# Strassen-Winograd FFN pairs: PSUM banks of a tile declared independent, and three columns done in the plain form

## The chip, the cores and the metric

The kernel runs on one core of a Trainium2 chip. The metric is the device time of one execution in microseconds (us); lower is better. Each core has a matrix engine (TensorE, PE in the profile, with its weight loads shown as PEld), a vector engine (VectorE, DVE), a scalar engine (ScalarE, ACT), GpSimd (POOL), and a queue engine (SyncE, SP) that issues the DMAs here. Matmul results go to PSUM, which has 8 banks of 512 fp32 values per partition. A PSUM tile of this kernel is 128 x 1024 fp32, two banks.

## The reference

Two transformer-like blocks on x of 1024 tokens by 1024 channels, all in fp32. What matters here is the last stage of the second block, a gated feed-forward network with a causal convolution of three taps between its two products:

```
z = rmsnorm(x) @ w_up                     # 1024 x 1024 by 1024 x 5632
zc = conv_b + sum over 3 taps of conv_w[tap] * z shifted by tap
gate, val = halves of zc                  # 2816 channels each
x = x + (silu(gate) * val) @ w_down       # 2816 x 1024
```

The 2816 gate channels are 22 columns of 128; column f of the gate and column f of val (f + 22 in `w_up`) make one of 22 tasks.

## The kernel before, in words

Precision: each fp32 operand is split into two fp32r numbers, hi (a ScalarE copy) and lo (VectorE: source minus hi; `hilo`, line 126 for the subtraction), and each product is three matmuls: hi by hi, lo by hi, hi by lo (`mm3`). A matmul is 128 x 128 weights by 512 columns of tokens.

Order: the kernel is a list of slots (`run`). A slot has weights, matmuls (`mm`), an epilogue (`epi`), and may take background tasks (`bg`: so many from the queue `bgq` after its matmuls; -1: all that are left) or work ahead of its matmuls (`mid`). Every engine executes its instructions in the order in which this list traces them. Weights of plain slots are loaded one or two slots ahead by SP (`dma_ahead`, tile `wr`), split by ScalarE and VectorE into `wh` and `wl` (`split_ahead`, two buffers each). `hold` on a slot sets `self.limit`, the number of weight requests that may be loaded before somebody lifts it.

Plain form of an FFN column: `mm_std`, 2 token halves x 8 blocks of channels x 3 matmuls = 48 for the gate and 48 for val, 96 together. Its epilogue `up_epi` runs `up_tasks`: ScalarE scales and biases the PSUM tile into `z`, VectorE adds two taps from PSUM (line 129), then silu (gate) or the product of gate and val, which SP writes to DRAM (`G_sp`, line 1643).

Columns 0 (gate and val) and 1 (gate) are done in half slots of 24 matmuls (`next_half_slots`, names uh0.0 to uh2.1), the first of them among the last slots of the stage before; up1.1 is a plain slot. Then come the pairs.

Pair form (`run_two`, columns 2 to 21 before): the product of two weight columns (gate and val) with the two token halves is done after Strassen and Winograd with 7 products in place of 8. Each product is 4 blocks x 3 matmuls = 12, so 84 for a pair. The weights' raw tile `raw` (`two_load`, line 311) gives sums (`two_sums`), and four parts a, b, c, d are split to hi and lo (`two_hi`, line 336, and `two_lo`); the tokens' sums are made once by `sums_of`, 16 background tasks in four groups of whole, first, second and split (tiles `f`, `s`, and the results in `A` and `B`), taken by the half slots. Products go into four banks, g1 and g2 of tile x, g3 and g4 of tile y. In order, with what VectorE and ScalarE do:

1. product 1 into g1 (weights a); ScalarE copies g1 to `e[:, 0]` (tile `two`)
2. product 6 into g2 (b); VectorE: `e[:, 1]` = g2 + `e[:, 0]`
3. product 5 into g3 (b); VectorE: `e[:, 2]` = g3 - `e[:, 0]`
4. product 2 onto g1 (a)
5. product 7 onto g2 (c); VectorE: g4 = `e[:, 2]` - g2
6. product 3 onto g3 (d); VectorE: g3 = g3 - `e[:, 1]`
7. product 4 onto g2 (c); VectorE: g2 = g2 + `e[:, 0]`

The texts below number the products by this order of issue, 1 to 7. The epilogue of a pair (`todo`) is woven into the next pair by `old`; the last pair runs its own at once. In the trace `wa`, `wb`, `wc` are the parts a, b, c, and part d lies in the tiles `A` and `B`, which also hold the tokens' hi and lo.

The way out: in the last pair `last_two` opens the pools of the plain form again in the place of wa and wb, and loads the first weights of the down projection. Then `open_d` loads the first gate products (`gr`), and `down` runs 2 x 22 column steps of 24 matmuls (names dn0.0 onward; the last two of each half in one slot) into all 8 PSUM banks.

Of the kernel before, what the change touches and what calls it, by code (L numbers as in the profile page):

```python
# [12 lines left out]
R = mybir.dt.float32r  # L13
AF = mybir.ActivationFunctionType
ALU = mybir.AluOpType
AX = mybir.AxisListType

S = 1024
D = 1024
NK = 8  # L20
H = 512
P = 128
NF = 22
# [50 lines left out]
class Kernel:  # L74
# [32 lines left out]
        self.c1 = self.ca.enter_context(self.pool(name, reuse_waits="tile"))  # L107

    def mul(self, *a, **k):
        self.nc.tensor.matmul(*a, **k)  # L110

    def flip(self, *a):
        self.nc.tensor.transpose(*a)  # L113
# [1 line left out]
    def act(self, out, in_, func=AF.Identity, bias=None, scale=None, accum=None):  # L115
        kw = {}
        if bias is not None:
            kw["bias"] = bias
        if scale is not None:
            kw["scale"] = scale  # L120
        if accum is not None:
            kw["accum_out"] = accum
        self.nc.scalar.activation(out, in_, func, **kw)  # L123

    def tt(self, out, a, b, op):
        self.nc.vector.tensor_tensor(out, a, b, op)  # L126

    def stt(self, out, a, s, b, op0, op1):
        self.nc.vector.scalar_tensor_tensor(out, a, s, b, op0, op1)  # L129
# [42 lines left out]

    def mm3(self, out, a, b, first, last, **k):
        (ah, al), (bh, bl) = a, b
        self.mul(out, ah, bh, start=first, stop=False, **k)
        self.mul(out, ah, bl, start=False, stop=False, **k)
        self.mul(out, al, bh, start=False, stop=last, **k)

    def mm_std(self, ps, w, xh, xl, nk=NK, k0=0, halves=(0, 1), xk0=0):
        wh, wl = w  # L180
# [175 lines left out]
    def run_two(self, n):  # L356
        t = self.twos[n]
        x, y = self.pair(), self.pair()
        g1, g2, g3, g4 = x[:, :H], x[:, H:], y[:, :H], y[:, H:]
        later = deque(self.twos[n - 1].todo if n else ())  # L360
        e = self.c1.tile([P, 3, H], F, tag="two", name="two")

        def product(out, op, which, off, first):
            (wh, wl), (xh, xl) = t.__dict__[which], self.X7[op]
            for k in range(4):
                ws = slice(off + k * P, off + (k + 1) * P)
                self.mm3(out, (wh[:, ws], wl[:, ws]), (xh[:, k], xl[:, k]),
                         first and k == 0, k == 3, skip_group_check=True)

        def old(k):  # L370
            for _ in range(min(k, len(later))):
                later.popleft()()

        product(g1, 1, "a", 0, True)
        self.two_hi(n, "c")
        old(2)
        self.act(e[:, 0], g1)
        product(g2, 6, "b", 0, True)
        old(1)
        self.two_lo(n, "c")  # L380
        self.two_hi(n, "d")
        self.tt(e[:, 1], g2, e[:, 0], ALU.add)
        product(g3, 5, "b", H, True)
        self.two_lo(n, "d")
        self.two_hi(n + 1, "a")
        self.two_sums(n + 1, 0)
        self.tt(e[:, 2], g3, e[:, 0], ALU.subtract)
        product(g1, 2, "a", H, False)
        if n == len(self.twos) - 1:
            self.last_two()  # L390
        self.two_load(n + 2)
        self.two_sums(n + 1, 1)
        self.two_lo(n + 1, "a")
        old(1)
        product(g2, 7, "c", 0, False)
        self.two_hi(n + 1, "b")
        old(2)
        self.tt(g4, e[:, 2], g2, ALU.subtract)
        product(g3, 3, "d", 0, False)
        self.two_lo(n + 1, "b")  # L400
        old(1)
        self.tt(g3, g3, e[:, 1], ALU.subtract)
        product(g2, 4, "c", H, False)
        old(len(later))
        self.tt(g2, g2, e[:, 0], ALU.add)
        t.todo = t.epi(x, y)
        if n == len(self.twos) - 1:
            for f in t.todo:
                f()
# [514 lines left out]
    def out_phase(self, blk):  # L924
        nc, I = self.nc, self.I
# [111 lines left out]
        def norm(t):  # L1037
            x, v = X[t], V[t]
            nc.vector.tensor_scalar(x, x, v[:, 0:1], v[:, 1:2], ALU.add, ALU.mult)
            self.tt(x, x, st["ln_g"], ALU.mult)  # L1040
            nc.gpsimd.tensor_tensor(x, x, st["ln_b"], ALU.add)
            nc.sync.dma_start(self.x1_sp[t], x)

        def scale(t):
            y = st["z", t] = self.c1.tile([P, 1024], F, tag="oz", name="oz", bufs=2)
            self.stt(y, X[t], V[t][:, 2:3], st["mix" if ln else "ffn"], ALU.mult, ALU.mult)
# [52 lines left out]
        def flip_slot(t):  # L1099
            add(Slot(mm=lambda: flips(t), name="fl"))  # L1100
# [3 lines left out]
        def then(f, *ts):  # L1104
            add(Slot(epi=lambda: [f(t) for t in ts]))

        nxt = self.next_half_slots(blk)
# [17 lines left out]
        if ln:  # L1125
            add(nxt[0])
            flip_slot(6)
            nxt[1].mid = lambda: norm(7)
            add(nxt[1])
            then(square, 7)  # L1130
            nxt[2].mid = lambda: scale(7)
            add(nxt[2])
            flip_slot(7)
            self.slots.extend(nxt[3:])
        else:
            then(scale, 7)
            add(nxt[0])
            flip_slot(7)
            add(Slot(pre=self.open_ffn))
            for x in nxt[1:]:  # L1140
                x.bg = 4
            self.slots.extend(nxt[1:])

    def next_half_slots(self, blk):
# [81 lines left out]
    def block2(self):  # L1226
# [135 lines left out]
        def att_a(n, kv):  # L1362
# [14 lines left out]
            def epi():  # L1377
# [8 lines left out]
                nm, es, tot = sm[:, 0], sm[:, 1], sm[:, 2]  # L1386
                nc.vector.tensor_reduce(nm, t[:, :, v], AX.X, ALU.max)
                self.tt(nm, nm, self.nslope[:, hs], ALU.mult)
# [205 lines left out]
    def open_ffn(self):  # L1594
        self.reopen("cf", "")
        self.wp = self.c1
        self.sh = [self.big(n, R).rearrange("p k (h t) -> p (k h) t", h=2).rearrange(
            "p (n k) t -> p n k t", n=4) for n in ("B1", "A0")]
        self.G_sp = self.dram.tile([NF, P, 1024], F, name="g_sp")
        wc = [self.wp.tile([P, 1024], R, name="wc%d" % j) for j in range(2)]  # L1600
        wa, wb = [[], []], []
        wd = [self.A1[:, 8192 + i * H:8192 + (i + 1) * H] for i in range(2)]
        count = [0]

        def tile(which):
            if which in "ab" and not wb:
                p, = self.open_right("wab")
                for i in range(2):
                    wa[i] += [p.tile([P, 1024], R, name="wa%d%d" % (i, j)) for j in range(2)]
                wb.extend(p.tile([P, 1024], R, name="wb%d" % j) for j in range(2))  # L1610
            if which == "a":
                count[0] += 1
                return wa[(count[0] + 1) % 2]
            return {"b": wb, "c": wc, "d": wd}[which]

        self.two_tile = tile
        self.X7 = self.operands(*self.H, self.sh)

        def scratch():
            return (self.wp.tile([P, 2, 1024], F, tag="raw", name="f", bufs=2),  # L1620
                    self.wp.tile([P, 4, H], F, tag="sums", name="s"))

        self.bgq.extend(self.sums_of(*self.H, self.sh, scratch))
        self.bgq.append(self.two_begin)
# [28 lines left out]
    def ffn(self):  # L1653
        nc, I = self.nc, self.I

        def mm3up(w):
            self.ps3 = self.pair()
            self.mm_std(self.ps3, w, *self.H)

        self.slots.append(Slot([I["w_up"][1 + NF]], mm3up, mid=self.last_half, bg=-1,  # L1660
                               epi=lambda: self.up_epi(1, 1, self.ps3), name="up1.1"))
        self.slots.append(Slot(pre=self.two_first))
        self.slots.append(Slot(pre=lambda: self.open_psum(4, 0)))

# [4 lines left out]
                return [g[0], g[1], g[2], lambda: (g[3](), v[0]()), v[1], v[2], v[3]]  # L1669
            return epi  # L1670

        for f in range(2, NF):
            slot = Slot(name="up%d" % f)
            slot.two = Two(I["w_up"][f], I["w_up"][f + NF], epi_of(f))
            self.slots.append(slot)
# [3 lines left out]
        def last_two():  # L1679
            _, self.first_g = self.open_right("ws", "g0")  # L1680
            t = st["g", 0, 0] = self.first_g.tile([P, H], F, name="gr0")
            nc.sync.dma_start(t, self.G_sp[0][:, 0:H])
            self.limit += 1
            self.split_ahead()

        self.last_two = last_two

        def down(hf, fs):
            hs = slice(hf * H, (hf + 1) * H)
# [47 lines left out]
            def epi():  # L1737
                if not end:
                    return
                for b in range(8):  # L1740
                    if b == 5 and hf == 0:
# [5 lines left out]

            self.slots.append(Slot([I["w_dn"][f] for f in fs], mm, epi, pre,
                                   split=[lambda f=f: split(f) for f in fs], name="dn%d.%d" % (hf, fs[0])))
            self.slots[-1].hold = True  # L1750

        def open_d():
            self.reopen("cd")
            self.limit = 1 << 30
            for f in range(1, 5):
                t = st["g", 0, f] = self.c1.tile([P, H], F, tag="gr", name="gr", bufs=6)
                nc.sync.dma_start(t, self.G_sp[f][:, 0:H])

        self.slots.append(Slot(pre=open_d))
        for hf in range(2):  # L1760
            for f in range(NF - 2):
                down(hf, (f,))
            down(hf, (NF - 2, NF - 1))
# [83 lines left out]
```

## Time and profile before

| | |
|---|---|
| median of 3 runs | 2848.7 us (2848.11 to 2849.38) |
| the profiled execution | 2853.09 us, span 2851.3 us |
| PE | 2741.4 us busy, 12180 matmuls |
| DVE, ACT | 1565.5 and 862.7 us busy |
| granted clock of PE | 0.99 of full on average |
| pairs | from about 2148 to 2586 us of the span |

The busy time of PE is made of modelled ends of pipelined matmuls, which overlap: a matmul shows 0.39 us of its own while the next starts some 0.23 us after it. Rows of the timeline give start, length, engine, line, operation, output and inputs, and in brackets the idle time before it and who ended it. A line is often that of a helper (110 all matmuls, 126 all two-input VectorE operations), so tiles tell the groups apart.

### The profile page before, as it was taken

What the parts mean: (1) busy time and instruction counts of PE and PEld (TensorE: products, weight loads), DVE (VectorE), ACT (ScalarE), POOL (GpSimd) and SP (SyncE); (2) the same over time, 40 slices, a digit from 0 to 9 for tenths busy, and PEclk for the clock granted to TensorE, in tenths of its full rate; (3) what the DMA queues carried; (4) which work ended last, traced back from release to release, by engine and by line L of the source; (5) the groups of instructions that cost most, each with busy time, mean ns of one, the idle gap of its engine ahead of it and who ended that gap; (6) DMA issues with size and microseconds to landing.
All of it is one profiled execution on the core that took longest, in us unless ns stands there. A gap on an engine that the chain in (4) does not pass through costs nothing.

```text
span 2851.3 us, 29350 instructions
## 1 busy us (share of the span) xinstructions
PE 2741.4 (96%) x12180; PEld 2239.4 (79%) x12180; DVE 1565.5 (55%) x1675; ACT 862.7 (30%) x1102; POOL 137.0 (5%) x131
## 2 busy tenths in 40 slices
PE   5999999999999999999999999999988999997999
PEld 3888888888888888888887888888866777775887
DVE  6898888831335323522662355457466777773343
ACT  6322222211222212411442355433233333332222
POOL 4010000000000000000041100000000000000000
PEclk9999999999999999999999999999989999998999
DMA  5111111122111333221422222024312112112544
GB/s 222 45 67 60 52 52 59 59 75 73 56 48 45 105 132 111 96 81 67 148 95 77 82 74 74 30 90 151 141 58 83 74 67 82 74 63 103 177 171 159
DMA packets 76167, 255.15 MB, mean 89 GB/s; under 512 B 8577, under 2 KB 9089, under 8 KB 76034
## 3 DMA queue, kind: packets, MB, share of 16 engines
q1 hardware_dynamic: 76034, 253.28, 25.1%
q8 instruction: 96, 1.57, 0.2%
q14 instruction: 37, 0.30, 0.0%
HBM read 208.15 MB, written 45.09 MB: 89 GB/s over the span
## 4 chain that ended last, share of the span: by engine, by line
PE 87%; DVE 7%; issue 2%; ACT 2%; DMA 1%; POOL 1%; SPq 0%; DVEq 0%; ACTq 0%; POOLq 0%
PE pp L110 85%; DVE z L129 2%; DVE wa L126 1%; PE pm L110 1%; PE pp L113 1%; PE pm L113 1%; DVE s L126 1%; DVE wl L126 1%; ACT oj L123 0%; DVE pp L126 0%; DVE A L126 0%; DVE two L126 0%; ACT two L123 0%; DVE sums L126 0%; ACT B L132 0%
## 5 line engine op out<-in xcount | busy, mean ns | idle before, releaser
L110 PE MATMUL pp<-A,wh 128*128 128x512 f32 x4192 | 1307.1, 392 | 19.1 <-DVE A L126 8.3
L110 PEld LDWEIGHTS pp<-A,wh 128*128 128x128 f32 x4192 | 786.3, 188 | 191.1 <-DVE A L126 9.9
L110 PE MATMUL pp<-A,wl 128*128 128x512 f32 x2128 | 832.5, 391 | 6.7 <-DVE wl L126 6.6
L126 DVE TENSOR_TENSOR wl<-wr,wh 128x1024 fp32r<-128x1024 f32 (+1 forms) x228 | 274.6, 1205 | 553.4 <-ACT wh L132 551.9
L110 PEld LDWEIGHTS pp<-A,wl 128*128 128x128 f32 x2128 | 401.6, 189 | 93.4 <-DVE wl L126 9.6
L132 ACT CAST wh<-wr 128x1024 fp32r<-128x1024 f32 (+1 forms) x228 | 229.9, 1009 | 423.5 <-PE pp L110 405.9
L129 DVE SCALAR_TENSOR_TENSOR h<-p,par_t,h 128x1024 f32<-128x1024 f32 x240 | 309.4, 1289 | 7.7
L110 PE MATMUL pp<-B,wh 128*128 128x512 f32 x960 | 303.6, 392 | 0.7 <-DVE sy L129 0.7
L110 PEld LDWEIGHTS pp<-B,wh 128*128 128x128 f32 x960 | 181.3, 189 | 38.5 <-issue 0.9
L110 PE MATMUL pp<-B,A 128*128 128x512 f32 x640 | 188.5, 399 | 23.6 <-DVE pp L126 23.2
L110 PE MATMUL pp<-B,wl 128*128 128x512 f32 x448 | 174.3, 389 | 0.0
L110 PEld LDWEIGHTS pp<-B,A 128*128 128x128 f32 x640 | 120.5, 189 | 57.4 <-issue 31.5
L110 PE MATMUL pp<-wh,gh 128*128 128x512 f32 x352 | 138.4, 393 | 15.1 <-ACT gh L132 9.7
L110 PE MATMUL pp<-wl,gh 128*128 128x512 f32 x352 | 138.5, 393 | 0.3 <-DVE wl L126 0.3
L110 PE MATMUL pp<-wh,gl 128*128 128x512 f32 x352 | 138.4, 393 | 0.1
L129 DVE SCALAR_TENSOR_TENSOR z<-pp,par_t,z 128x1023 f32<-128x1023 f32 x88 | 112.7, 1281 | 39.4 <-ACT z L123 37.8
L126 DVE TENSOR_TENSOR mg<-pp,mg 128x1024 f32<-128x1024 f32 x24 | 29.4, 1224 | 168.2 <-PE pp L110 168.2
L110 PE MATMUL pp<-B,wb 128*128 128x512 f32 x320 | 105.7, 402 | 13.8 <-ACT two L123 13.8
L110 PE MATMUL pp<-A,wa 128*128 128x512 f32 x320 | 107.1, 396 | 5.1 <-DVE z L129 4.0
L110 PEld LDWEIGHTS pp<-B,wl 128*128 128x128 f32 x448 | 84.1, 188 | 17.4
L123 ACT ACTIVATE mg<-pp,par_t 128x1024 f32<-128x1024 f32 x24 | 26.8, 1117 | 219.8 <-PE pp L110 219.8
L110 PEld LDWEIGHTS pp<-wh,gh 128*128 128x128 f32 x352 | 66.7, 190 | 30.5 <-ACT gh L132 10.5
(265 smaller groups left out, 2952.6 us busy)
## 6 DMA issues: line engine op xcount, KB each, us to landing
wr<-in_w_in SPq DMA_DIRECT2D x129, 512.0 KB, 3.2
wr<-in_w_dn SPq DMA_DIRECT2D x44, 512.0 KB, 3.4
raw<-in_w_up SPq DMA_DIRECT2D x40, 512.0 KB, 4.5
wr<-in_w_br SPq DMA_DIRECT2D x24, 512.0 KB, 3.5
g_sp<-z SPq DMA_DIRECT2D x22, 512.0 KB, 2.6
gr<-g_sp SPq DMA_DIRECT2D x44, 256.0 KB, 3.8
m_sp<-mg SPq DMA_DIRECT2D x16, 512.0 KB, 2.9
mi<-m_sp SPq DMA_DIRECT2D x16, 512.0 KB, 5.0
```

Of the source, the lines that this page charges most:

```text
L110: self.nc.tensor.matmul(*a, **k)
L113: self.nc.tensor.transpose(*a)
L123: self.nc.scalar.activation(out, in_, func, **kw)
L126: self.nc.vector.tensor_tensor(out, a, b, op)
L129: self.nc.vector.scalar_tensor_tensor(out, a, s, b, op0, op1)
L132: self.nc.scalar.copy(hi, src)
```

## The change

The helpers `mul`, `act` and `tt` return the instruction that they make, and `mm3` a list of three. In `run_two` every instruction of the seven products and of the VectorE and ScalarE steps is noted under its bank. For two instructions on different engines (one of them PE) in different banks of the same tile it is declared that they do not depend on each other; between instructions in the same bank an explicit dependence is added.

Columns 2, 3 and 21 are done in the plain form: 2 and 3 ahead of the pairs and 21 behind them; 17 pairs are left (4 to 20). The 16 background tasks and the first raw loads are taken by the half slots as 2, 2, 1, 1, 1 (4 each before), by the four plain slots that follow as 2 each, and the rest by the last. `last_two` now lifts the limit altogether and splits one weight, that of column 21; `hold` moves from the down slots to the plain slot of column 21. The tiles wa, wb are allocated in an order that depends on the number of pairs.

```diff
     def mm3(self, out, a, b, first, last, **k):
         (ah, al), (bh, bl) = a, b
-        self.mul(out, ah, bh, start=first, stop=False, **k)
-        self.mul(out, ah, bl, start=False, stop=False, **k)
-        self.mul(out, al, bh, start=False, stop=last, **k)
+        return [self.mul(out, ah, bh, start=first, stop=False, **k),
+                self.mul(out, ah, bl, start=False, stop=False, **k),
+                self.mul(out, al, bh, start=False, stop=last, **k)]
...
+        seen = {1: [], 2: [], 3: [], 4: []}
+        other = {1: 2, 2: 1, 3: 4, 4: 3}
+
+        def apart(bank, insts, after=()):
+            for i in insts:
+                for o in seen[other[bank]]:
+                    if (o.ins.engine == PE) == (i.ins.engine == PE):
+                        continue
+                    self.tc.declare_no_dep(i.ins, o.ins, reason="other bank")
+            for o in after:
+                self.tc.add_manual_dep(insts[0].ins, o.ins.name, mybir.DependencyInfo(
+                    mybir.DependencyClass.Sync, mybir.DependencyReason.DATA), reason="same bank")
+            seen[bank] += insts
+
-        def product(out, op, which, off, first):
+        def product(bank, op, which, off, after=()):
             (wh, wl), (xh, xl) = t.__dict__[which], self.X7[op]
+            out, insts = banks[bank], []
             for k in range(4):
                 ws = slice(off + k * P, off + (k + 1) * P)
-                self.mm3(out, (wh[:, ws], wl[:, ws]), (xh[:, k], xl[:, k]),
-                         first and k == 0, k == 3, skip_group_check=True)
+                insts += self.mm3(out, (wh[:, ws], wl[:, ws]), (xh[:, k], xl[:, k]),
+                                  not after and k == 0, k == 3, skip_group_check=True)
+            apart(bank, insts, after)
+            return insts[-1]
+
+        def vec(bank, inst, after):
+            apart(bank, [inst], [after])
+            return inst
...
-        product(g1, 1, "a", 0, True)
+        banks = {1: g1, 2: g2, 3: g3, 4: g4}
+        m1 = product(1, 1, "a", 0)
...
-        self.act(e[:, 0], g1)
-        product(g2, 6, "b", 0, True)
+        c1 = vec(1, self.nc.scalar.copy(e[:, 0], g1), m1)
+        m2 = product(2, 6, "b", 0)
...
-        self.tt(e[:, 1], g2, e[:, 0], ALU.add)
-        product(g3, 5, "b", H, True)
+        v2 = vec(2, self.tt(e[:, 1], g2, e[:, 0], ALU.add), m2)
+        m3 = product(3, 5, "b", H)
...
-        self.tt(e[:, 2], g3, e[:, 0], ALU.subtract)
-        product(g1, 2, "a", H, False)
+        v3 = vec(3, self.tt(e[:, 2], g3, e[:, 0], ALU.subtract), m3)
+        product(1, 2, "a", H, [c1])
...
-        product(g2, 7, "c", 0, False)
+        m2 = product(2, 7, "c", 0, [v2])
...
-        self.tt(g4, e[:, 2], g2, ALU.subtract)
-        product(g3, 3, "d", 0, False)
+        v2 = self.tt(g4, e[:, 2], g2, ALU.subtract)
+        apart(2, [v2], [m2])
+        apart(4, [v2])
+        m3 = product(3, 3, "d", 0, [v3])
...
-        self.tt(g3, g3, e[:, 1], ALU.subtract)
-        product(g2, 4, "c", H, False)
+        vec(3, self.tt(g3, g3, e[:, 1], ALU.subtract), m3)
+        m2 = product(2, 4, "c", H, [v2])
         old(len(later))
-        self.tt(g2, g2, e[:, 0], ALU.add)
+        vec(2, self.tt(g2, g2, e[:, 0], ALU.add), m2)
...
-            for x in nxt[1:]:
-                x.bg = 4
+            for x, n in zip(nxt[1:], (2, 2, 1, 1, 1)):
+                x.bg = n
...
-                for i in range(2):
-                    wa[i] += [p.tile([P, 1024], R, name="wa%d%d" % (i, j)) for j in range(2)]
-                wb.extend(p.tile([P, 1024], R, name="wb%d" % j) for j in range(2))
+                last = (len(self.twos) + 1) % 2
+                for x, i in ((wa[1 - last], "a0"), (wb, "b"), (wa[last], "a1")):
+                    x.extend(p.tile([P, 1024], R, name="w%s%d" % (i, j)) for j in range(2))
...
-        def mm3up(w):
-            self.ps3 = self.pair()
-            self.mm_std(self.ps3, w, *self.H)
-
-        self.slots.append(Slot([I["w_up"][1 + NF]], mm3up, mid=self.last_half, bg=-1,
-                               epi=lambda: self.up_epi(1, 1, self.ps3), name="up1.1"))
+        up = {}
+
+        def plain(f, side, bg=0):
+            def mm(w):
+                up[f, side] = self.pair()
+                self.mm_std(up[f, side], w, *self.H)
+
+            slot = Slot([I["w_up"][f + NF * side]], mm, bg=bg, name="up%d.%d" % (f, side),
+                        epi=lambda: self.up_epi(f, side, up[f, side]))
+            self.slots.append(slot)
+            return slot
+
+        plain(1, 1, 2).mid = self.last_half
+        for f, side, bg in ((2, 0, 2), (2, 1, 2), (3, 0, 2), (3, 1, -1)):
+            plain(f, side, bg)
         self.slots.append(Slot(pre=self.two_first))
...
-        for f in range(2, NF):
+        for f in range(4, NF - 1):
...
             nc.sync.dma_start(t, self.G_sp[0][:, 0:H])
-            self.limit += 1
-            self.split_ahead()
+            self.limit = 1 << 30
+            self.split_ahead(1)

         self.last_two = last_two
+        plain(NF - 1, 0).hold = True
+        plain(NF - 1, 1)
...
-            self.slots[-1].hold = True

         def open_d():
             self.reopen("cd")
-            self.limit = 1 << 30
```

More of the change, by code (lines that the diff above doesn't have):

```diff
@@ L16 @@
 AX = mybir.AxisListType
+PE = mybir.EngineType.PE
 S = 1024
@@ L109, in mul @@
     def mul(self, *a, **k):
-        self.nc.tensor.matmul(*a, **k)
+        return self.nc.tensor.matmul(*a, **k)
     def flip(self, *a):
@@ L122, in act @@
             kw["accum_out"] = accum
-        self.nc.scalar.activation(out, in_, func, **kw)
+        return self.nc.scalar.activation(out, in_, func, **kw)
     def tt(self, out, a, b, op):
-        self.nc.vector.tensor_tensor(out, a, b, op)
+        return self.nc.vector.tensor_tensor(out, a, b, op)
     def stt(self, out, a, s, b, op0, op1):
```

## The prediction

> **What bounds the kernel now.** I read the page first, then the busy time by stretches, then who waited for whom inside the FFN pairs, then the instructions of one pair, then the two ends of the pairs.
>
> ```profile
> span 2851.3 us, 29350 instructions
> PE 2741.4 (96%) x12180; PEld 2239.4 (79%) x12180; DVE 1565.5 (55%) x1675; ACT 862.7 (30%) x1102; POOL 137.0 (5%) x131
> ```
>
> TensorE is the bound, but its 96% hides gaps, because the modelled ends of matmuls overlap what comes next. The number of matmuls in a stretch says more (columns: length, busy time and count of PE, PEld, DVE, ACT, POOL, then the granted clock).
>
> ```profile
> 200.00:400.00 200.00, 200.00 (x884) 165.62 (x883) 168.10 (x135) 47.20 (x44) 19.38 (x16) 1.00 0.17 58
> 2085.00:2150.60 65.60, 47.87 (x170) 35.72 (x169) 49.08 (x43) 21.30 (x18) 0.00 (x0) 0.84 0.19 66
> 2191.40:2553.64 362.24, 333.33 (x1429) 265.38 (x1429) 271.70 (x290) 126.70 (x136) 0.00 (x0) 1.00 0.19 72
> 2553.64:2607.67 54.03, 34.15 (x132) 26.23 (x133) 23.61 (x24) 11.93 (x14) 0.00 (x0) 0.84 0.24 83
> ```
>
> A stretch of plain projections issues 884 matmuls in 200 us: 0.2262 us each, my price of a matmul throughout. The second row is the way into the pairs (170 matmuls, worth 38.5 us, in 65.6), the third is 17 whole pairs, the fourth the way out (132, worth 29.9 us, in 54.0). All three lose time, and the change touches all three.
>
> The steady pairs (who waited for whom: total us, times, longest) and one of them, with the start of the sixth product in two pairs 17 apart:
>
> ```profile
> DVE z L129 <- ACT z L123: 22.7, 17, 1.3
> PE pp L110 <- DVE pp L126: 17.2, 17, 1.0
> DVE two L126 <- PE pp L110: 16.1, 34, 0.7
> PE pp L110 <- ACT two L123: 11.7, 17, 0.7
> ...
> 2191.40 8.46 PE pp L110 x36
> 2553.64 8.46 PE pp L110 x36
> ...
> 2306.00 0.39 PE L110 MATMUL pp<-A,wa 128*128 128x512 f32 x1
> 2307.08 0.50 PE L110 MATMUL pp<-B,wb 128*128 128x512 f32 x1 [0.69 <-ACT two L123]
> ...
> 2317.86 0.39 PE L110 MATMUL pp<-B,wc 128*128 128x512 f32 x1
> 2319.26 0.47 PE L110 MATMUL pp<-B,A 128*128 128x512 f32 x1 [1.01 <-DVE pp L126]
> ...
> 2303.71 0.70 DVE L126 TENSOR_TENSOR pp<-pp,two 128x512 f32<-128x512 f32 x1 [2.02 <-PE pp L110]
> 2318.43 0.69 DVE L126 TENSOR_TENSOR pp<-two,pp 128x512 f32<-128x512 f32 x1
> ```
>
> The period is (2553.64 - 2191.40) / 17 = 21.31 us. A pair has 7 products of 12 matmuls, 84 x 0.2262 = 19.00. The missing 2.31 us are two waits, each once a pair. Product 2 (weights wb, into g2) waits for ScalarE's copy out of g1, the other bank of tile x: 1.08 us between starts instead of 0.23. Product 6 (weights d, in A and B, into g3) waits for VectorE's write of g4, the other bank of tile y: 1.40 instead of 0.23. That is 0.85 + 1.17, and about 0.1 twice for the first matmul after each wait. Neither needs what it waits for: wb, wc and d were ready.
>
> **The change, part by part.**
>
> *Banks declared apart, 17 pairs.* Both waits go, since product 2 touches no bank of the copy and product 6 none of the g4 write. What is late next? The g4 write reads g2 and must be done before product 7, one product (12 x 0.2262 = 2.71 us) later than now. VectorE goes from 2303.71 (g2 of the pair before) to 2319.12 (end of the g4 write) with two idle spells on PE of 0.47 mean (the 16.1 us over 34), so 15.41 - 0.95 = 14.46 us of its queue, 1.33 of it a wait for ScalarE's z. Product 1 starts at 2303.51; unbroken, product 5 ends at 2303.51 + 13.57 + 0.17 = 2317.25, VectorE is free for g4 at 2317.48, writes until 2318.17, and product 7 is due at 2319.79: 1.6 us to spare. Closed into a loop (14.46, then product 7 with its drain, about 3.0) VectorE's chain needs 17.5 us, under 19.00. Its busy time, 271.70 / 17 = 16.0, fits as well. So PE sets 19.00; bounds 19.0 and 21.3 (nothing won), nearest to the plain stretch's rate, hence 19.0. The added same-bank waits (copy before product 4, and so on) look back at least one product and cost nothing under that cover.
>
> There is a published figure to weigh. The Trainium skill (TensorE: Matmul & The Clock Gate, Back-to-back issue gap) gives about 131 ns per N=512 matmul sustained in a stream with weight loads and 215.7 ns for an isolated gap. The trace has 226.2 in stretches without a wait, so it agrees with the second within 5% and not with the first; at 215.7 a pair would be 18.1 us and 17 pairs 15 us shorter than I say. The row decides.
>
> *Columns 2 and 3 plain, sums spread.* Now each 24-matmul half slot (5.43 us) is followed by four background tasks:
>
> ```profile
> PE pp L110 <- DVE wl L126: 6.4, 4, 1.8
> PE pp L110 <- ACT wh L132: 6.2, 3, 3.3
> ...
> 2087.46 2.29 DVE L126 TENSOR_TENSOR f<-A,B 128x2048 f32<-128x2048 f32 x1
> 2089.79 1.29 DVE L126 TENSOR_TENSOR s<-f 128x512 f32<-128x512 f32 x2
> 2091.00 1.41 DVE L126 TENSOR_TENSOR s<-s,f 128x512 f32<-128x512 f32 x2
> 2094.39 2.29 DVE L126 TENSOR_TENSOR A<-s,B 128x2048 fp32r<-128x2048 f32 x1 [1.98 <-ACT B L132]
> 2096.60 1.22 DVE L126 TENSOR_TENSOR wl<-wr,wh 128x1024 fp32r<-128x1024 f32 x1
> 2118.25 2.60 DVE L129 SCALAR_TENSOR_TENSOR z<-pp,par_t,z 128x1023 f32<-128x1023 f32 x2
> ```
>
> One group of four with its wait for ScalarE and the next wl fills VectorE from 2087.46 to 2097.8, 10.3 us against 5.43. PE waits, and the clock falls (0.84 above). With 2, 2, 1, 1, 1 tasks there, VectorE owes in the five half slots: five wl 6.1, two f 4.6, two s<-f 2.6, two s<-s,f 2.8, one A with its wait 4.3, two pairs of taps 5.2, one product of z 1.2 (as at 2595.90 below), total 26.8 against 27.1. Put in order from 2087.46, behind each slot's start on PE, the wl for the slots that start at 2095.9, 2101.3, 2106.8 and 2112.2 end at about 2092.7, 2099.4, 2103.6 and 2110.7, each before it is wanted, so no wait; lower bound 0, upper bound the 4.9 us per slot that is owed now, once: 5. In the five long slots (10.86 each) the most is about 11.3 in one, 6.4 in the next. ScalarE's casts lie inside the 1.98 us wait and beside VectorE's work. The weight loads sit on SP behind the writes of z, but each is asked for a slot ahead; the two raw loads, asked for in column 3's second slot, have over 10 us until the pairs.
>
> PE's work from 2084.8 is then 120 + 48 + 192 = 360 matmuls, 81.4 us, to 2166.2. Then comes the old hand-over, unchanged in kind: after the last plain column ScalarE's z, two taps and the product stand ahead of wa.
>
> ```profile
> 2143.91 0.39 PE L110 MATMUL pp<-A,wl 128*128 128x512 f32 x1
> 2148.32 0.76 PE L110 MATMUL pp<-A,wa 128*128 128x512 f32 x1 [4.02 <-DVE z L129]
> 2150.62 1.22 PE L110 MATMUL pp<-A,wa 128*128 128x512 f32 x2 [1.11 <-DVE wa L126]
> ...
> 2170.02 0.47 PE L110 MATMUL pp<-B,A 128*128 128x512 f32 x1 [0.88 <-DVE pp L126]
> ```
>
> From the end at 2144.14 to the third matmul: 6.48 us. From there to product 6, 19.40 us where 58 x 0.2262 = 13.1 would do; 2.0 are the two waits, 4.3 the slow clock after the gap. I keep 6.48 and 4.3. So the third matmul is at 2172.7, pair 0 ends 82 x 0.2262 + 4.3 later at 2195.5, and 16 more pairs at 2499.5.
>
> *The way out, column 21 plain.* Now, with PE's waits, the dn weights and the tail of the epilogue (gr is the load of gate products for the down phase):
>
> ```profile
> PE pp L110 <- ACT gh L132: 9.7, 1, 9.7
> PE pp L110 <- DVE z L129: 5.3, 2, 3.2
> PE pp L110 <- DVE pp L126: 4.1, 1, 4.1
> ...
> 2586.15 0.39 PE L110 MATMUL pp<-wh,gh 128*128 128x512 f32 x1
> 2607.67 0.79 PE L110 MATMUL pp<-wh,gh 128*128 128x512 f32 x1 [9.75 <-ACT gh L132]
> ...
> 2586.35 0.70 DVE L126 TENSOR_TENSOR pp<-pp,two 128x512 f32<-128x512 f32 x1 [2.12 <-PE pp L110]
> 2595.90 1.23 DVE L126 TENSOR_TENSOR z<-z 128x1024 f32<-128x1024 f32 x1
> ...
> 2597.57 2.32 SPq L1757 DMA_DIRECT2D gr<-g_sp  x4
> ...
> 2607.00 0.61 ACT L132 CAST gh<-gr 128x512 fp32r<-128x512 f32 x1
> ...
> gr<-g_sp SPq DMA_DIRECT2D x44, 256.0 KB, 3.8
> ```
>
> The first down slot starts at 2586.15, but needs PSUM of the last pair; the second starts at 2607.67, 21.5 us later for 5.43 of work. The last pair's own epilogue ran 10.8 us (2586.35 to 2597.13) with nothing beside it. After: 96 matmuls (21.7 us) of column 21 cover that epilogue. Its weights are the price: the wh of the last pair's split now lies over wb, free after product 3, not product 4, so the 4.1 us wait before product 6 goes too. Column 21's second half finds its wl queued behind the epilogue: 10.8 + 1.2 + 0.2 after the pair's end against 10.86 + 0.45 of PE work, a wait of 0.9. Its end: 2499.5 + 21.7 + 0.9 = 2522.1. First down slot 5.43, whose last PSUM pair is free 4.1 us in and wanted then: 2527.6. The second needs gr 1, which SP issues only behind the write of z: taps 4.1, product 1.2, two issues 0.5, landing 3.8, gh 0.6, gl 0.7 less two matmuls: 10.4 after column 21's end, 5.0 more than 5.43. Bounds: 0 if the load comes early, 10 as now. I take 5.0. The dn weight loads are now asked for ahead of that write (the limit is lifted in last_two), so they no longer add the 6 us. Second slot: 2532.6, with the same slow restart as now.
>
> *Sum.* 2607.67 - 2532.6 = 75.1 us saved: pairs 17 x 2.31 = 39, and 36 at the two ends, where three columns cost 0.4 us each as plain ones (21.71 against 21.31) and stalls of about 37 us go. The profiled execution took 2853.1 us, span 2851.3; it becomes 2778.0. The median of the runs shown is 4.4 us below it: 2848.7 - 75.1 = 2773.6.
>
> **The rivals.** (1) The declarations do not take effect, for instance because another dependence between the same instructions remains: pairs stay at 21.31, only the ends win 36, 2813. For it: the waits are made by the framework, not shown in the trace; against: the two rows name just the instructions declared apart. (2) One wait stays or VectorE's loop, 1.5 us from the bound, stretches to about 20.2: 17 x 1.2 = 20, 2794. For: VectorE is at 75% already and will be at 84%. (3) Slower or no gain: the same loop, with VectorE's queue now holding waits between product ends, would have to grow from 17.5 to over 19.0 + 75.1 / 17 = 23.4 us per pair; below that there is a gain. Nothing in the rows lengthens an instruction by a third. (4) PE, once nothing interrupts it, issues faster than in any row, until VectorE's loop of 17.5 us bounds the pair: 17 x 1.5 = 25 us less, 2748; the plain stretches, without a wait and at 0.2262, speak against it. (By the Trainium skill's sustained figure, cited above from TensorE: Matmul & The Clock Gate, Back-to-back issue gap, that would be the case.)
>
> **How the numbers follow.** Forecast 0.80, rival 1 0.07, rival 2 0.09, rival 3 0.03, rival 4 0.01. Predicted 2774. Low end: the 5.0 us at the second down slot gone and 2 us of slow clock, 2767. High end: 5 us at the way in, 5 at the way out, 0.6 per pair, about 2794, which takes in rival 2 in part. A difference of 0.2% (5.7 us) is about what a measurement of this kernel can tell. Only rival 3 lies above: faster 0.96, same 0.02, slower 0.02.
>
> **What would show it.** Right: no waits of PE for ACT two or DVE pp in the pairs, starts of product 6 19.0 us apart; 360 matmuls in about 82 us ahead of the hand-over at clock 1.00; the second down slot about 10 us after column 21. Wrong: a period over 19.5 with PE waiting for the g4 write at product 7 (rival 2), the old 0.69 and 1.01 still there (rival 1), PE waiting for wl in the first plain slots, or a wait for gh longer than 5 us.

## The result, and the profile after

The changed kernel takes 2774.81 us (median of 4 runs, 2772.83 to 2775.40) against 2849.04 us before it (2848.11 to 2852.44): the ratio is 0.9736, with a 95% interval from 0.9719 to 0.9753. The forecast was 2774 us.

The page of the changed kernel, its first lines:

```profile
span 2773.0 us, 29379 instructions
PE 2724.6 (98%) x12216; PEld 2244.0 (81%) x12216; DVE 1540.3 (56%) x1645; ACT 856.3 (31%) x1093; POOL 136.9 (5%) x131
```

There are 36 matmuls more than before (three columns with 96 in place of 84), and yet 78 us of span less. Busy time by stretches (length, then busy time and count of PE, PEld, DVE, ACT, POOL, the granted clock, the DMA share and GB/s): plain projections, the way in, the first pair, 16 pairs, the way out.

```profile
200.00:400.00 200.00, 200.00 (x884) 165.69 (x883) 168.09 (x135) 47.20 (x44) 19.38 (x16) 1.00 0.17 58
2083.60:2171.80 88.20, 83.10 (x366) 68.03 (x363) 66.21 (x57) 32.28 (x29) 0.00 (x0) 0.98 0.24 86
2171.80:2193.43 21.63, 21.63 (x83) 17.71 (x84) 12.85 (x15) 5.28 (x7) 0.00 (x0) 0.86 0.18 66
2193.43:2498.07 304.64, 304.64 (x1345) 252.41 (x1344) 249.39 (x269) 117.85 (x127) 0.00 (x0) 1.00 0.22 82
2498.07:2530.87 32.80, 27.66 (x121) 22.01 (x119) 17.53 (x16) 10.85 (x12) 0.00 (x0) 0.98 0.26 87
```

The 16 pairs issue 1345 matmuls in 304.64 us, 0.2265 us each: the rate of the plain stretch, which had been the assumption. From the way in to the way out PE waits four times (in each row: us in total, times, longest), where before it waited 40 times for the two causes inside the pairs alone. First the pairs before, then the whole stretch after (gh is the hi part of the gate products gr):

```profile
PE pp L110 <- DVE pp L126: 23.2, 20, 4.1
PE pp L110 <- ACT two L123: 13.8, 20, 0.7
```

```profile
PE pp L111 <- ACT gh L133: 4.5, 1, 4.5
PE pp L111 <- DVE wa L127: 2.9, 1, 2.9
PE pp L111 <- ACT wa L337: 2.2, 1, 2.2
PE pp L111 <- DVE wl L127: 0.7, 1, 0.7
```

One pair of the changed kernel, in the timeline. Product 2 (weights wb) starts ahead of ScalarE's copy out of the other bank; the g4 write now runs beside product 6 (weights d, shown as A and B), and product 7 (wc) starts without a gap.

```profile
2462.28 0.39 PE L111 MATMUL pp<-A,wa 128*128 128x512 f32 x1
2462.51 0.39 PE L111 MATMUL pp<-B,wb 128*128 128x512 f32 x1
...
2462.71 0.59 ACT L401 COPY two<-pp 128x512 f32<-128x512 f32 x1 [0.72 <-PE pp L111]
...
2473.39 0.39 PE L111 MATMUL pp<-B,A 128*128 128x512 f32 x1
...
2473.73 0.68 DVE L127 TENSOR_TENSOR pp<-two,pp 128x512 f32<-128x512 f32 x1
...
2475.88 0.39 PE L111 MATMUL pp<-B,A 128*128 128x512 f32 x1
2476.11 0.39 PE L111 MATMUL pp<-A,wc 128*128 128x512 f32 x1
...
2481.75 0.59 ACT L401 COPY two<-pp 128x512 f32<-128x512 f32 x1 [0.72 <-PE pp L111]
```

The copies are 2481.75 - 2462.71 = 19.04 us apart: the period, 21.31 before. The g4 write ends at 2474.41, 1.7 us ahead of product 7.

### The profile page after: what moved, and what is told of

It is laid out like the page before. It is cut to its first block, busy times and chain, and to the rows that moved or that the text cites. A ratio compares the mean times of both kernels' runs of the same rounds, so it can differ in the third digit from the quotient of the medians.

```text
span 2773.0 us, 29379 instructions
## 1 busy us (share of the span) xinstructions
PE 2724.6 (98%) x12216; PEld 2244.0 (81%) x12216; DVE 1540.3 (56%) x1645; ACT 856.3 (31%) x1093; POOL 136.9 (5%) x131
## 4 chain that ended last, share of the span: by engine, by line
PE 93%; DVE 3%; issue 1%; ACT 1%; POOL 1%; DMA 1%; SPq 0%; DVEq 0%; ACTq 0%; POOLq 0%
PE pp L111 91%; PE pm L111 1%; PE pp L114 1%; PE pm L114 1%; ACT oj L124 0%; DVE wl L127 0%; DVE A L127 0%; DVE z L130 0%; POOL ox L1067 0%; DVE ox L127 0%; DVE B L481 0%; DVE s L127 0%; DMA B<-in_xt 0%; DMA wr<-in_w_out 0%; ACT z L124 0%
## 5 line engine op out<-in xcount | busy, mean ns | idle before, releaser
L111 PE MATMUL pp<-A,wh 128*128 128x512 f32 x4288 | 1341.9, 391 | 12.9 <-DVE A L127 8.3
L111 PEld LDWEIGHTS pp<-A,wh 128*128 128x128 f32 x4288 | 803.1, 188 | 186.3 <-DVE A L127 9.9
L111 PE MATMUL pp<-A,wl 128*128 128x512 f32 x2224 | 867.7, 390 | 1.0 <-DVE wl L127 0.9
L127 DVE TENSOR_TENSOR wl<-wr,wh 128x1024 fp32r<-128x1024 f32 (+1 forms) x234 | 281.9, 1205 | 550.2 <-ACT wh L133 546.8
L111 PEld LDWEIGHTS pp<-A,wl 128*128 128x128 f32 x2224 | 418.3, 188 | 89.4 <-DVE wl L127 2.3
L111 PE MATMUL pp<-B,wh 128*128 128x512 f32 x1056 | 338.4, 390 | 0.0
L111 PEld LDWEIGHTS pp<-B,wh 128*128 128x128 f32 x1056 | 197.9, 188 | 40.5
L111 PE MATMUL pp<-B,A 128*128 128x512 f32 x616 | 176.9, 393 | 0.4 <-DVE B L127 0.3
L111 PE MATMUL pp<-A,wa 128*128 128x512 f32 x272 | 91.4, 398 | 5.1 <-DVE wa L127 2.9
L111 PE MATMUL pp<-B,wb 128*128 128x512 f32 x272 | 87.1, 392 | 0.0
```

The lines of the kernel that those rows point to most:

```text
L111: return self.nc.tensor.matmul(*a, **k)
L127: return self.nc.vector.tensor_tensor(out, a, b, op)
```

## The experiments

The kernel before ran again beside each group of these runs (medians from 2849.1 to 2850.6 us), the changed kernel did not. Differences are to its 2774.8 us unless said, and one or two us of such a difference say nothing.

**Each half of the change alone.** The banks declared apart in the kernel before. With the declarations come only the explicit same-bank dependences and another form of ScalarE's copy (COPY in place of ACTIVATE, 0.59 us against 0.60):

```diff
     (the kernel before; run_two, mul, tt and mm3 of the changed kernel)
-        self.act(e[:, 0], g1)
-        product(g2, 6, "b", 0, True)
+        c1 = vec(1, self.nc.scalar.copy(e[:, 0], g1), m1)
+        m2 = product(2, 6, "b", 0)
...
```

> The kernel before with the banks declared apart and nothing else: 20 pairs, four background tasks in each half slot, the old way out. If the pairs' gain stands on its own: the product-to-product period falls from 21.31 to 19.0, 19 periods x 2.27 = 43, and the last pair's 4.1 us wait of PE for the g4 write becomes one of about 1.4 before product 7 and may spare its 2.9 us of slow clock: 45 to 51 us, so about 2801. Rival: the ends carry the change and the pairs give their waits back elsewhere (at product 7, or as waits for weights): period above 20, time above 2820.

Measured: 2800.46 us, ratio to before 0.9827 (0.9811 to 0.9843), 50.1 us less than the 2850.56 of the kernel before beside it. Two copies of successive pairs are 19.04 us apart; below them, the one wait for VectorE that is left, that of the last pair:

```profile
2458.99 0.59 ACT L401 COPY two<-pp 128x512 f32<-128x512 f32 x1 [0.72 <-PE pp L111]
2478.03 0.59 ACT L401 COPY two<-pp 128x512 f32<-128x512 f32 x1 [0.72 <-PE pp L111]
```

```profile
PE pp L111 <- DVE pp L127: 1.3, 1, 1.3
```

19 pairs give 19 x 2.27 = 43.1. In the last one the wait for the copy goes (1.0), the wait for VectorE falls from 4.1 to 1.3 (2.8), and the matmuls behind it, 0.43 us apart before, are 0.23 us apart from the second on (2.7). That makes some 49.6 of the 50.1 us. The pairs' gain stands on its own.

The other half, without the declarations:

```diff
-                    self.tc.declare_no_dep(i.ins, o.ins, reason="other bank")
+                    pass
```

> The changed kernel without the declarations (the explicit same-bank dependences stay, columns 2, 3 and 21 stay plain). If the gain is pairs plus ends: period 21.3 again, 17 x 2.27 = 39 us over the changed kernel, about 2813.5. If the declarations do nothing and the ends alone explain the gain: 2775.

Measured: 2813.06 us (2812.64 to 2814.28), 38.3 more. Both waits are back, 17 times each:

```profile
PE pp L111 <- DVE pp L127: 17.8, 17, 1.6
PE pp L111 <- ACT two L401: 11.5, 17, 0.7
```

So the waits came from dependences between different banks, which the declarations remove (against rival 1 of the prediction). The new form of the copy is in this kernel too, so it is not what removes them.

**The two waits apart.** The declarations for one tile only, here tile x alone (for tile y alone the new condition is `bank < 3`):

```diff
-                    if (o.ins.engine == PE) == (i.ins.engine == PE):
+                    if bank > 2 or (o.ins.engine == PE) == (i.ins.engine == PE):
```

> The changed kernel with the declarations for banks 1 and 2 (tile x) alone. The wait before product 2 is gone, the one before product 6 for the g4 write stays, and VectorE's queue is now the later one there: 1.1 to 1.3 us a pair, period 20.2, 17 x 1.2 = 20 us over the changed kernel, about 2795. If the two waits were one chain (the second only passes the first on): about 2775 or about 2813.

> The changed kernel with the declarations for banks 3 and 4 (tile y) alone. The wait before product 2 for ScalarE's copy stays, 0.85 + 0.1 us a pair, period 20.0, 17 x 0.95 = 16 us over the changed kernel, about 2791. If the waits add up, this and the kernel with tile x alone share 37 to 39 us; if one hides behind the other, their sum is less.

Measured, one run each: tile x alone 2796.07 us (21.3 more), tile y alone 2789.93 (15.1 more). The rows below are from the chain of work that ended last (start, length, engine, number of matmuls). In each kernel the two starts are at the same product of two successive pairs; first tile x alone, then tile y alone:

```profile
2330.85 13.90 PE pp L111 x60
2351.19 13.86 PE pp L111 x60
```

```profile
2316.74 19.35 PE pp L111 x84
2336.76 19.35 PE pp L111 x84
```

Periods of 20.34 and 20.02 us, 1.30 and 0.98 over 19.04. They add up to 2.28, which is the 21.31 - 19.04 of both, and 21.3 + 15.1 = 36.4 us is within 2 us of the 38.3 of both. The waits are separate, and the one on VectorE's write is the dearer.

**How much VectorE has to spare.** One or two operations more per pair ahead of the g4 write:

```diff
+        if n + 1 < len(self.twos):
+            s = self.twos[n + 1].sums[:, 0:2].rearrange("p n c -> p (n c)")
+            for _ in range(1):                      # or 2
+                junk = self.c1.tile([P, 1024], F, tag="junk", name="junk")
+                self.tt(junk, s, s, ALU.add)
         v2 = self.tt(g4, e[:, 2], g2, ALU.subtract)
```

> The changed kernel with one VectorE operation more in each of 16 pairs, ahead of the g4 write (an addition of 128 x 1024 into a tile that nobody reads, about 1.15 us of the queue). The theory that PE is the bound with 1.5 to 1.7 us of VectorE's loop to spare: period stays 19.04, time 2775. Rival, that the loop is already the bound or has less to spare: period 19.3 to 20.2, 2779 to 2793.

> The same with two such operations (about 2.3 us). The theory: the loop of 17.5 us becomes 19.7 to 19.8, so the period is 19.7 to 19.8 and PE waits before product 7 for the g4 write, 16 x 0.7 = 11 us, about 2786. If VectorE's total busy time is the limit and not the loop (16.0 + 2.3 = 18.3, under 19.0): 2775. If the slack is nil: 16 x 2.3 = 37, 2812.

Measured, one run each: 2772.19 us with one (nothing is lost), 2787.64 with two (12.8 more). The idle time of VectorE ahead of its operations on PSUM, one such wait a pair: 16 of them in the changed kernel, 15 in the kernel with one operation more. Then, with two, the wait of PE, two starts in the chain one pair apart, and the new operation:

```profile
DVE pp L127 <- PE pp L111: 28.1, 16, 2.0
```

```profile
DVE pp L127 <- PE pp L111: 9.1, 15, 0.6
```

```profile
PE pp L111 <- DVE pp L127: 9.0, 15, 0.6
```

```profile
2210.01 11.21 PE pp L111 x48
2229.96 11.21 PE pp L111 x48
```

```profile
L127 DVE TENSOR_TENSOR junk<-sums x32: 1214/1221/1227, 2185.3 to 2487.4; 128x1024 f32<-128x1024 f32 x32
```

The first operation is eaten whole by the idle time (1.76 us a pair becomes 0.61). The second makes VectorE's loop the bound (its work from one g4 write through product 7 to the next), with the period at 19.95: 2 x 1.2 us back from there is a loop of 17.5, as worked out from the kernel before. Its total busy time (249.39 / 16 = 15.6 us a pair, and 2.4 more, 18 of 19.04) would have fitted; it is the loop through product 7 that counts. So the pairs are 1.5 us from the point where VectorE takes over.

**The way in and the way out, each as before.** Columns 2 and 3 as pairs with four background tasks in each half slot; and column 21 as a pair, with the old `last_two`, places and limits:

```diff
-            for x, n in zip(nxt[1:], (2, 2, 1, 1, 1)):
+            for x, n in zip(nxt[1:], (4, 4, 4, 4, 4)):
...
-        for f, side, bg in ((2, 0, 2), (2, 1, 2), (3, 0, 2), (3, 1, -1)):
-            plain(f, side, bg)
...
-        for f in range(4, NF - 1):
+        for f in range(2, NF - 1):
```

> The changed kernel with the old way in: columns 2 and 3 as pairs (19 pairs), four background tasks in each half slot. The theory: the stalls and the slow clock of the half slots come back (65.6 - 38.0 - 6.5 = 21.1 us), less two columns that cost 19.04 as pairs and 21.7 as plain ones (5.3): 15.8 us over the changed kernel, about 2790.5. Rival, that the way in was not VectorE-bound: about 5 us below the changed kernel, 2769.5.

```diff
-        for f in range(4, NF - 1):
+        for f in range(4, NF):
...
-            self.limit = 1 << 30
-            self.split_ahead(1)
+            self.limit += 1
+            self.split_ahead()
...
-        plain(NF - 1, 0).hold = True
-        plain(NF - 1, 1)
```

> The changed kernel with the old way out: column 21 as a pair (18 pairs), one weight let through by the limit in the last pair, the old places of wa and wb. The theory: from the end of the last pair to the second down slot 21.5 us instead of 32.8, and a pair of 19.04 more, 1.4 us or more of wait before its product 7: 9 to 12 us over the changed kernel, 2784 to 2787. Rival, that the down phase gives the time back later (its loads or the clock): within 3 us of the changed kernel.

Measured: 2790.28 us (2 runs, 15.5 more) and 2784.84 us (2 runs, 10.0 more). The waits of PE that came back, of the old way in and of the old way out:

```profile
PE pp L111 <- ACT wh L133: 7.4, 2, 5.0
PE pp L111 <- DVE wl L127: 7.1, 5, 1.8
```

```profile
PE pp L111 <- ACT gh L133: 9.7, 1, 9.7
PE pp L111 <- DVE z L130: 5.4, 2, 3.3
...
PE pp L111 <- DVE pp L127: 1.3, 1, 1.3
```

The parts close: 50.1 us for the declarations in all 20 pairs, 15.5 for the way in and 10.0 for the way out are 75.6. The whole is 75.8 from the same 2850.56 us, and 74.2 from the 2849.04 of the result.

**What is left at the two ends.** Two gaps remain. The first is at the second down slot: its gh waits for a load of gate products that SP issues behind the write of column 21. GpSimd issues it instead:

```diff
                 t = st["g", 0, f] = self.c1.tile([P, H], F, tag="gr", name="gr", bufs=6)
-                nc.sync.dma_start(t, self.G_sp[f][:, 0:H])
+                nc.gpsimd.dma_start(t, self.G_sp[f][:, 0:H])
```

> The changed kernel with the first four gate-product loads of the down phase issued by GpSimd, which is idle there, instead of SP, where they stand behind the write of column 21. The theory that SP's order makes the 4.5 us wait for gh at the second down slot: the loads land tens of us earlier, the slot then waits for VectorE's wl and gl only (about 1.1 us), and the slow clock after the wait (about 3.3 us) is spared too: 5 to 7 us less, about 2768.5. Rival, that the place of the loads (the tiles they go into come free late) is what holds them: no change, 2775.

Measured: 2768.70 us (2767.97 to 2769.55), 6.1 less. In the changed kernel, the write of column 21 and the issue of the loads right behind it on SP; then, in this one, the issue and PE in the second down slot:

```profile
2525.93 0.33 SPq L1669 DMA_DIRECT2D g_sp<-z  x1
2526.31 2.22 SPq L1792 DMA_DIRECT2D gr<-g_sp  x4
```

```profile
2497.28 2.42 POOL L1792 DMA_DIRECT2D gr<-g_sp  x4 [416.17 <-PE pp L111]
...
2525.14 0.39 PE L111 MATMUL pp<-wh,gh 128*128 128x512 f32 x1
2526.00 0.50 PE L111 MATMUL pp<-wl,gh 128*128 128x512 f32 x1 [0.47 <-DVE wl L127]
```

The tiles are free when the last pair ends (2497.28), some 29 us before the time of SP's turn (2526.31): it was the order on SP, not the place. Of the 4.46 us wait 0.47 is left, for wl. From the last pair's end to the second down slot the profiled execution is 4.6 us shorter than the changed kernel's; another 1.3 are slow clock in its first pair, which this edit does not touch.

The second gap is the hand-over to the pairs:

```diff
-        self.bgq.append(self.two_begin)
+        self.bgq.insert(len(self.bgq) - 1, self.two_begin)
...
-            plain(f, side, bg)
-        self.slots.append(Slot(pre=self.two_first))
+            s = plain(f, side, bg)
+        s.epi = lambda: (self.two_first(), self.up_epi(3, 1, up[3, 1]))
...
-                for x, i in ((wa[1 - last], "a0"), (wb, "b"), (wa[last], "a1")):
+                for x, i in ((wa[last], "a0"), (wb, "b"), (wa[1 - last], "a1")):
...  (last_two: dma_ahead() only; split_ahead(1) after the last pair's step 6)
```

> The changed kernel with the first pair's weights prepared before the epilogue of column 3 and not after it (wa of the first pair placed over the raw tiles, and so the last pair's first load after its product 4, its split after product 6). The theory that the 6.4 us hand-over is the epilogue's place in the queues, and that the slow clock after it (4.3 us) follows from the gap: the hand-over shrinks to 1 to 2 us and the slow clock goes, 8 to 10 us less, about 2766. Rival, that the pair's PSUM or weight tiles come free only with column 3's end and epilogue: 0 to 3 us less.

> Both of these edits. If the two gaps are apart, the gains add: about 15 us less than the changed kernel, 2759 to 2761.

Measured: 2766.99 us (2766.29 to 2768.01), 7.8 less, just under the 8 to 10 expected, and both together 2761.63 us (2761.27 to 2763.34), 13.2 less than the changed kernel and 0.9691 of the time before (0.9676 to 0.9705). In the kernel with the earlier weights the last plain matmul, the first of the pair and its only wait; then the clock in the same 21 us there and in the changed kernel:

```profile
2164.55 0.39 PE L111 MATMUL pp<-A,wl 128*128 128x512 f32 x1
2164.78 0.39 PE L111 MATMUL pp<-A,wa 128*128 128x512 f32 x1
...
2168.67 0.73 PE L111 MATMUL pp<-B,wb 128*128 128x512 f32 x2 [0.53 <-DVE wb L127]
```

```profile
2164.00:2185.00 21.00, 20.47 (x91) 16.54 (x90) 17.00 (x20) 6.41 (x8) 0.00 (x0) 1.00 0.20 75
```

```profile
2164.00:2185.00 21.00, 15.90 (x55) 12.13 (x54) 14.64 (x16) 7.23 (x8) 0.00 (x0) 0.76 0.20 72
```

No gap, and the clock stays at 1.00: 91 matmuls in place of 55. The gain of both is a little short of the sum (13.2 against 13.9, and the 15 expected), which is within the spread of the runs: with the hand-over gone the other queue is worth 5.4 us (2766.99 to 2761.63). From the first half slot to the down phase PE of this last kernel is without a gap worth naming:

```profile
2083.00:2530.00 447.00, 445.24 (x1963) 367.55 (x1962) 349.91 (x359) 169.68 (x177) 2.40 (x4) 1.00 0.24 88
```

## Why the prediction was right, step by step

- *Pairs.* The period was to be 19.00 and is 19.04; both named waits went, in every pair, and nothing took their place. The 1.6 us to spare for the g4 write is 1.7 in the trace, and the loop of 17.5 us was found by adding work. The division of the 2.31 us (0.95 for the copy, 1.27 for the write) is 0.98 and 1.30.
- *The published matmul figure.* 0.2265 us a matmul in unbroken pairs settles it: the Trainium skill's figure of about 216 ns for an isolated gap (TensorE: Matmul & The Clock Gate, Back-to-back issue gap) is 5% under, its 131 ns for a sustained stream does not occur here. Rival 4 is out.
- *The way in.* No wait for wh or wl in the plain slots. The chain of waits has PE alone in it there, and again from the third matmul of the first pair to the end of the seventeenth (1426 = 82 + 16 x 84 matmuls). The last row is that stretch in the kernel with the gate loads on GpSimd, whose code up to there is the same:

```profile
2083.82 81.63 PE pp L111 x360
...
2171.76 326.29 PE pp L111 x1426
```

```profile
2171.93 325.02 PE pp L111 x1426
```

 81.4 was the price for the 360 matmuls. The hand-over was to take 6.48 us and does (2165.28 to 2171.76).
- *Slow clock of the first pair.* The term that was mis-sized: 4.3 us taken over from before, 2.9 in the profiled execution. From the third matmul to product 6, over 58 matmuls, it takes 16.03 us (2171.76 to 2187.79) where 58 x 0.2265 = 13.14 would do. It is no fixed price: by the same measure it was 1.6 us in the kernel of the last row above, and between 1.6 and 3.0 in the seven kernels here that keep the 6.5 us hand-over and have no other wait up to product 6. Why it varies stays open.
- *The way out.* From the last pair's end to the second down slot 33.1 us were worked out, 33.0 are measured, with both waits in it (2497.87 to 2530.87; 0.9 for wl forecast, 0.67 of idle time in the trace; 5.0 for gh, 4.46).
- *Sum.* 75.1 us forecast in the span; the medians differ by 74.2, the two profiled spans by 78.3. Of the 3.2 us between forecast and spans 1.2 lie ahead of the change: the stage before ends at 2083.82 in place of 2085.00, and in the runs above it moves by up to 2 us without being touched. The slow clock is another 1.4, and 1.5 lie behind the second down slot, which was forecast to restart as before (242.1 us to the end, 243.6 before); against them the 16 periods took 0.6 more than forecast. That the median came within 1 us of 2774 is thus in part luck: the executions of one kernel differ by 2 to 5 us, and the profiled one before was 4 us above its median, the one after was at it.

## What to carry to other kernels

A dependence that is tracked by tile and not by bank shows up as one short wait per use, always the same, for an engine that reads or writes the other half. It costs little each time and much in a loop: price it by start-to-start times against the unbroken rate, since the busy share hides it. Before removing it, work out which engine's loop comes next and how far away it is; here it was 1.5 us. And work that is less clever but independent (a plain column with 12 matmuls more) pays where it covers what had nothing beside it.

## What the runs showed of the hardware

A gap does not cost its own length alone, and what it costs on top varies. After the 6.5 us hand-over PE ran at half rate for a while (matmuls 0.43 us apart in place of 0.226), which took 4.3 us of extra time in the kernel before, 2.9 in the changed one and 1.6 in the one with the gate loads on GpSimd, after the same gap; waits of 0.5 to 1.1 us in the pairs left the clock at 1.00. The Trainium skill (TensorE: Matmul & The Clock Gate, What's actually happening) says that the clock follows a free-running window of about 3.4 us, which would make the extra time depend on where the gap falls; these runs agree with that, but do not test it.

ScalarE can read and VectorE can write one PSUM bank while PE writes the other bank of the tile, at no cost that these traces show: beside matmuls that start 0.23 us apart the copy takes 0.59 us (0.60 before, as an ACTIVATE) and the g4 write 0.69 on the median, as in the kernel before, where PE stood still for both.
